# Router logits in four column groups of the tensor engine, and another order of the first loads

## The chip, the cores and the metric

The kernel runs on one core of a Trainium2 chip. The metric is the device time of one execution in microseconds (us), as the median of several runs. The engines are TensorE (PE, matmuls; its weight loads are shown apart as PEld), VectorE (DVE), ScalarE (ACT), GpSimd (POOL) and SyncE (SP), which here only issues DMAs. PE reads SBUF and writes PSUM.

## The reference

One encoder block over a sequence of 1024 tokens with 1024 channels, in fp32:

```python
mod = silu(c) @ w_ada + b_ada                     # 6 parts of 1024
sh1, sc1, g1, sh2, sc2, g2 = split(mod, 6)

h = rmsnorm(x, norm_mix_g) * (1 + sc1) + sh1
u_f, q, k, v = split(h @ w_in)                    # 512 | 512 | 128 | 128 columns
q, k = rmsnorm per head                           # 8 query heads, 2 key/value heads of 64
y_f = fourier_mix(u_f)                            # 2-D DFT, real part, and a linear map per group
y_a = windowed_gqa(q, k, v, rel_bias, sink)       # +-128 tokens, blocks of 128 queries
x = x + g1 * (concat(y_f, y_a) @ w_out)

h2 = rmsnorm(x, norm_ffn_g) * (1 + sc2) + sh2
aff = softmax(h2 @ w_router)                      # 1024 tokens x 16 experts
g, idx = top_k(aff.T, 128)                        # each expert picks its 128 tokens
y_e = (silu(h2[idx] @ w_gate) * (h2[idx] @ w_up)) @ w_down * g
x = x + g2 * scatter_add(y_e)
```

## The kernel before

Tokens lie in 8 tiles of 128. The work has four stages.

1. **First pair of tiles** (`t0` to the first `in_order`). SP loads the identity and small rows, `x` tiles 0 and 1 (512 KB each, `load_x`, L223), the modulation weights of `sh1` and `sc1` and the projection weights `w_in` (`load_w`, L317, 640 KB for each of 8 channel chunks, called w0 to w7 here). The modulation weights come in 8 pieces of 1 MB (`load_mod`, L239, two DMAs of 512 KB each); piece 0 belongs to channel chunk 0, piece 1 to chunk 1, and later pieces come in pairs for two chunks. They are called modulation columns here. `mod_mac` (L127) multiplies such a column with silu(c) in four column groups of PE (32 output partitions each); `mod_sum` copies the result out (ACT, L253) and adds the groups with a matmul against ones (L255); `mod_cols` (DVE, L261 to L263) makes the scale `G1c` and shift `sh1c` of the chunk. `rms` (L193 to L196) squares a tile on ACT, makes the power on POOL, and DVE scales the tile (L355). `pair_chunk` transposes a chunk of both tiles (L271), applies scale and shift (ACT, L278, `hf`) and splits it into a rounded part `hh` and a remainder `hl`; `w_hi` and `w_lo` split the weights in the same way (L397, L321). `terms` (L376) is then the projection, three products for each chunk. The in-order pass at the end of this stage (`in_order(t0, *PINNED)`) holds all five engines to the order in which the program is written, so a statement moved in the source is moved in every engine's queue. The raw tiles of the modulation columns are four buffers, filled again as they are used up.
2. **The other six tiles**, one after the other, with the key and query norms and the rest of the modulation in the background.
3. **Attention, Fourier mixing, output projection, router.** Attention goes through 16 units (tile, key/value head), `front` and `back`; `tick` lets a filler advance in between. The filler is the Fourier part first. After unit 4 (`n == NSW`) the pool `p3` is opened and the filler is `filler2`, which takes the tiles through `oproj` (L81 to L83: three matmuls for each of 8 chunks and two halves). In `oproj(t)`, after the fourth chunk of the first half, `tail(t - 1)` makes the router's logits of the tile before: `x2_flip` transposes its residual (L834) and ACT copies it to `x2T` (L835); eight fp32 matmuls with `x2T` as the stationary operand and `wrG` (router weights times the norm's scale, 16 columns) as the moving one (L850) give 128 tokens x 16 logits in PSUM; DVE applies the token's factor (L852), then softmax into `aff`. For the last tile, `oproj(7)` calls `tail(t, 1)`, where the first four of the eight matmuls (L844) are done ahead. `sorter` sorts the affinities of finished tiles on DVE. Order within this stage is that of the tile framework's planner, which ranks instructions by its own costs; only the lines with `issue_after` are tied. `pt()` gives one of two PSUM buffers that transposes, router and others share.
4. **Experts.** `choose` and `gather` pick tokens for expert 0 (a gap for PE), then 16 experts run on PE with weights split by ACT (L86) and DVE (L87), 1 MB loads for each quarter of a matrix, released by buffers, and in program order on all engines.

An fp32 matmul shows as two records on PE and two weight loads on PEld.

Of the kernel before, what the change touches and what calls it, by code (L numbers as in the profile page):

```python
# [11 lines left out]
F32 = mybir.dt.float32  # L12
# [3 lines left out]
AF = mybir.ActivationFunctionType  # L16
OP = mybir.AluOpType
AX = mybir.AxisListType
# [7 lines left out]
NE = 16  # L26
# [19 lines left out]
def block_kernel(ctx: ExitStack, tc: tile.TileContext, t_in, out):  # L46
    nc = tc.nc
    PE, ACT, DVE, POOL, SP = nc.tensor, nc.scalar, nc.vector, nc.gpsimd, nc.sync

    x = t_in["x"][0]  # L50
# [5 lines left out]
    def pool(name, bufs=1, space=None, **kw):  # L56
        if space is None:
            return tc.tile_pool(name=name, bufs=bufs, reuse_waits="tile", **kw)
        return tc.tile_pool(name=name, bufs=bufs, space=space, **kw)
# [4 lines left out]
    def spacer(p, n):  # L64
        if n:
            p.tile([128, n // 4], F32, name=f"spacer{next(spaced)}", bufs=1)
# [6 lines left out]
    def pt(name="pt"):  # L73
        return ps.tile([128, 512], F32, name=name, tag="pt", bufs=2)
# [14 lines left out]
    def raw(shape):  # L89
        return raw1.tile(shape, F32, name="raw", tag="raw")  # L90


    ident = cst.tile([128, 128], F32, name="ident")
# [47 lines left out]
    def drain(g):  # L141
        for _ in g:
            pass
# [46 lines left out]
    def rms(pool_, src, name, tag, bufs, eng=None):  # L190
        junk = pool_.tile([128, D], BF, name="junk", tag=tag, bufs=bufs)
        ss = pool_.tile([128, 1], F32, name=name + "s", bufs=3)
        ACT.activation(junk, src, AF.Square, accum_out=ss)  # L193
        (eng or DVE).tensor_scalar(ss, ss, 1.0 / D, EPS, op0=OP.mult, op1=OP.add)
        rs = pool_.tile([128, 1], F32, name=name + "r", bufs=3)
        POOL.tensor_tensor(rs, ss, mhalf[:, 0:1], op=OP.pow)  # L196
        return rs
# [7 lines left out]
    p1 = p_a.enter_context(pool("p1"))  # L205
# [10 lines left out]
    xs, xr = {}, {}  # L216

    def stage():
        return p1.tile([128, 1280], F32, name="ws", bufs=2)

    def load_x(t):
        xs[t] = p1.tile([128, D], F32, name="xt", bufs=4)
        SP.dma_start(xs[t], x[t * 128:(t + 1) * 128, :])  # L223
# [9 lines left out]
    def load_mod(h):  # L233
        ks, j, n = halves[h]
        w = len(ks) * 128
        u = raw([128, n, 2, w])
        for i, part in enumerate((1, 0)):
            c0 = part * 1024 + ks[0] * 128
            SP.dma_start(u[:, :, i, :], w_ada_v[:, j:j + n, c0:c0 + w])  # L239
        mods[h] = u.rearrange("p j a c -> p j (a c)")  # L240
# [16 lines left out]
    def mod_cols(*ks):  # L257
        mp = msums.pop(ks)
        n = len(ks)
        c = slice(ks[0], ks[0] + n)  # L260
        DVE.tensor_tensor(G1c[:, c], mp[:, 0:2 * n:2], bscc[:, c], op=OP.add)  # L261
        DVE.tensor_tensor(G1c[:, c], G1c[:, c], ng1c[:, c], op=OP.mult)
        DVE.tensor_tensor(sh1c[:, c], mp[:, 2 * n:4 * n:2], bshc[:, c], op=OP.add)  # L263
# [51 lines left out]
    def load_w(kc):  # L315
        r = u_hi.rearrange("p a b -> p (a b)")[:, :1280] if kc % 3 == 2 else stage()
        SP.dma_start(r, w_in_v[:, kc, :])  # L317
        return r
# [8 lines left out]
    SP.dma_start(rows[0:16], b_ada[:, 0:2048].rearrange("l (j p) -> (l j) p", p=128))  # L327
    SP.dma_start(rows[16:24], t_in["norm_mix_g"].rearrange("l (j p) -> (l j) p", p=128))
    SP.dma_start(rows[24:28], t_in["b_fourier"].rearrange("l (j a) d -> (l j) (a d)", a=2))
    load_x(0)  # L330
    load_x(1)
    load_mod(0)
    load_mod(1)
    wraw = {0: load_w(0)}
    load_mod(2)
    load_mod(3)
    wraw[1] = load_w(1)
    wraw[2] = load_w(2)

    rb = p1.tile([32, 8], F32, name="rb")  # L340
# [2 lines left out]
    pw = p_w.enter_context(pool("pw"))  # L343
    for k in range(8):
        w_h[k], w_l[k] = ((pw if k < 4 else p1).tile([128, 1280], F32R, name=f"w{x}{k}") for x in "hl")
    rs0 = rms(p1, xs[0], "x", tag="hf", bufs=2, eng=POOL)
    rs1 = rms(p1, xs[1], "x", tag="hf", bufs=2, eng=POOL)
    p = pt()
    PE.transpose(p[:, :28], rows[:28], ident[:28, :28])
    DVE.tensor_copy(cols.rearrange("p a b -> p (a b)")[:, :28], p[:, :28])  # L350
    DVE.tensor_scalar(bscc, bscc, 1.0, None, op0=OP.add)
    mod_mac(0)
    mod_sum(0)
    for t, r in enumerate((rs0, rs1)):
        DVE.tensor_scalar(xs[t], xs[t], r, None, op0=OP.mult)  # L355
    mod_cols(0)

    bg, ada, dfts = [], [], []

# [79 lines left out]
    p = terms(pair, 0, hs.pop(0), 0)  # L439
# [64 lines left out]
    for m, (t, kc0) in enumerate(seq):  # L504
# [18 lines left out]
        for a in range(4):  # L523
            project((t,), kc0 + a, hs_, a * 128)
            if m == 0 and a == 1:
                DVE.scalar_tensor_tensor(gg, qg, HD ** -0.5, kg, op0=OP.mult, op1=OP.mult)
                p = pt()
# [309 lines left out]
    def tail(t, b0=0):  # L837
        x2, rs = x2s.pop(t)
        p = None
        for b in range(b0, 2):  # L840
            if b0:
                p = pt()
                for kc in range(4):
                    PE.matmul(p[:, :16], x2Ts[t][:, kc, :], wrG[:, kc, :], start=(kc == 0), stop=False)  # L844
            x2_flip(t, b, x2)
            yield
        x2T = x2Ts.pop(t)
        p = p or pt()
        for kc in range(4 * b0, 8):
            PE.matmul(p[:, :16], x2T[:, kc, :], wrG[:, kc, :], start=(kc == 0), stop=(kc == 7))  # L850
        lg = p3.tile([128, 16], F32, name="lg", bufs=2)
        DVE.scalar_tensor_tensor(lg, p[:, :16], rs, cb, op0=OP.mult, op1=OP.add)  # L852
        mx = p3.tile([128, 1], F32, name="mx", bufs=2)
        DVE.tensor_reduce(mx, lg, axis=AX.X, op=OP.max, negate=True)
        sm = p3.tile([128, 1], F32, name="sm", bufs=2)
        ex = p3.tile([128, 16], F32, name="ex", bufs=2)
        ACT.activation(ex, lg, AF.Exp, bias=mx, accum_out=sm)
        rsm = p3.tile([128, 1], F32, name="rsm", bufs=2)
        DVE.reciprocal(rsm, sm)
        after["aff"] = DVE.tensor_scalar(aff[:, t, :], ex, rsm, None, op0=OP.mult)  # L860
        ready.append(t)
        yield

    def router_prep():
        n2 = p3.tile([64, 128], F32, name="sb_", bufs=1)[:24]
        SP.dma_start(n2[0:8], md[1:2, :].rearrange("l (j p) -> (l j) p", p=128))
        SP.dma_start(n2[8:16], md[2:3, :].rearrange("l (j p) -> (l j) p", p=128))
        SP.dma_start(n2[16:24], t_in["norm_ffn_g"].rearrange("l (j p) -> (l j) p", p=128))
        p = pt()
        PE.transpose(p[:, :24], n2, ident[:24, :24])  # L870
        c2 = p3.tile([128, 24], F32, name="c2")
        DVE.tensor_copy(c2, p[:, :24])
        DVE.scalar_tensor_tensor(c2[:, 8:16], c2[:, 8:16], 1.0, c2[:, 16:24], op0=OP.add, op1=OP.mult)
        p = pt()
        for kc in range(8):
            PE.matmul(p[0:1, :16], c2[:, kc:kc + 1], wr[:, kc, :], start=(kc == 0), stop=(kc == 7))
        row = p3.tile([1, 16], F32, name="row")
        DVE.tensor_copy(row, p[0:1, :16])
        DVE.tensor_tensor(wrG, wr, c2[:, 8:16, None].to_broadcast([128, 8, 16]), op=OP.mult)
        p = pt()  # L880
        PE.matmul(p[:, :16], ones[0:1, :128], row, start=True, stop=True)
        DVE.tensor_copy(cb, p[:, :16])
# [94 lines left out]
    ydone, x2s, x2Ts, xts, ylive = {}, {}, {}, {}, [0]  # L977
    fr, qks, ready, sp = {}, {}, [], [None]
    srt = sorter()
    po, p3 = None, None  # L980
# [18 lines left out]
    for n in range(len(units) + 2):  # L999
        if n == NSW:  # L1000
            for _ in fill[0]:
                for g in lateq:
                    next(g, None)
            for g in lateq:
                drain(g)
            p_f.close()
            p_u.close()
            po = p_c.enter_context(pool("po"))
            p3 = p_c.enter_context(pool("p3", side="right"))
            sp[0] = p3  # L1010
            spacer(p3, 0)
            g1_r, sh2_r, G2_r = (p3.tile([128, D], F32, name=n_) for n_ in ("g1_r", "sh2_r", "G2_r"))
            wr, wrG = (p3.tile([128, 8, NE], F32, name=n_) for n_ in ("wr", "wrG"))
            cb = p3.tile([128, NE], F32, name="cb")
            load_x2(0)
            for i, r in enumerate((g1_r, sh2_r, G2_r)):
                SP.dma_start(r, md[i:i + 1, :].to_broadcast([128, D]))
            wo_h.append(po.tile([128, 2, D], F32R, name="woh3"))
            wo_l.append(po.tile([128, 2, D], F32R, name="wol3"))
            wo_cut()  # L1020
            wo_cut()
            fill = [filler2()]
            SP.dma_start(wr, t_in["w_router"][0].rearrange("(k p) e -> p k e", p=128))
        fg = front(*units[n]) if n < len(units) else iter(())
        bg = back(*units[n - 2]) if n >= 2 else iter(())
        next(fg, None)
        next(bg, None)
        next(fg, None)
        next(bg, None)
        next(bg, None)  # L1030
        drain(fg)
        for g in lateq:
            for _ in range(9):
                next(g, None)
        if n + 1 < len(units):
            qprep(*units[n + 1])
            tick()
        drain(bg)
# [283 lines left out]
    for k0, n in ((0, 2), (2, 2), (4, 4)):  # L1322
        p = pt()
# [119 lines left out]
```

## Time and profile before

| | us |
|---|---|
| median of 3 runs (lowest, highest) | 993.34 (992.99, 994.31) |
| profiled execution, whole | 994.39 |
| its span, first to last instruction | 992.1 |
| PE busy in the span | 938.7 |
| DVE, ACT, POOL busy | 788.6, 626.2, 403.3 |
| mean granted TensorE clock | 0.978 |

In the rows, `L850 PE MATMUL pt<-wrG,x2T 128*128 128x16 f32 x112` reads: line 850, engine PE, output tile `pt` from `wrG` and `x2T`, a 128x128 stationary operand, a 128x16 moving one, 112 records; then busy us and the mean ns of one, then the idle time of the engine just before them and what ended it. In rows by time the first two numbers are the start and the busy time in us, and what stands in brackets is the idle time before the row and what ended it. Rows of stretches give the stretch, its length, the busy us of each engine with the number of instructions, then the granted TensorE clock, the share of the DMA engines and GB/s.

### The profile page before, as it was taken

To read this page: it belongs to the slowest core of one execution; us is meant where nothing else is said; L and a number is where in the kernel's file an instruction comes from. 1 tells how busy PE (TensorE), PEld (TensorE's weight loads), DVE (VectorE), ACT (ScalarE), POOL (GpSimd) and SP (SyncE) were. 2 spreads that over 40 slices of the span, in tenths; PEclk is the share of its full clock that TensorE was granted. 3 is DMA by queue.
4 is the path that set the end of the run, shared out by engine and by line. 5 is a ranking of instruction groups with operands and counts; after the bars stand their busy time and mean duration, and the time that the engine had idled before them with its cause. 6 is when DMAs were issued, how large, how long until landed. Compare 5 with 4: busy or idle time off the path is not lost.

```text
span 992.1 us, 13155 instructions
## 1 busy us (share of the span) xinstructions
PE 938.7 (95%) x4737; PEld 745.1 (75%) x4737; DVE 788.6 (79%) x1237; ACT 626.2 (63%) x831; POOL 403.3 (41%) x239
## 2 busy tenths in 40 slices
PE   4999999979999999599899999999999999999996
PEld 2678776747787777358788888888888888888885
DVE  1336787778767969889879988988998898899894
ACT  2464534666555653137577787787778777777872
POOL 1007465100000000101348769767876976782201
PEclk9999999989999999599899999999999999999998
DMA  9977566362222148799989999999999999999922
GB/s 290 329 259 271 176 213 226 120 190 79 75 75 96 61 145 309 283 405 371 378 307 398 384 385 410 386 386 399 397 389 384 410 385 387 401 395 383 386 84 42
DMA packets 91641, 283.95 MB, mean 286 GB/s; under 512 B 8140, under 2 KB 25728, under 8 KB 91448
## 3 DMA queue, kind: packets, MB, share of 16 engines
q1 hardware_dynamic: 86712, 266.32, 70.6%
q0 software_dynamic: 4864, 16.80, 6.6%
q8 instruction: 37, 0.61, 0.2%
q14 instruction: 28, 0.23, 0.1%
HBM read 263.79 MB, written 21.40 MB: 287 GB/s over the span
## 4 chain that ended last, share of the span: by engine, by line
PE 56%; DMA 1%; DVE 1%; issue 0%; POOLq 0%; ACT 0%; DVEq 0%
PE pa L81 17%; PE pa L83 17%; PE pa L82 17%; PE pt L1290 3%; PE pa L1249 2%; DMA out_dram<-ys,idx 1%; DMA xe<-h2d,idx 0%; DVE wl L87 0%; PE pt L1271 0%; PE pt L1325 0%; POOLq L1439 0%; DVE oneh L1263 0%; DVE ys L1307 0%; PE pa L1135 0%; DVE t1l L87 0%
## 5 line engine op out<-in xcount | busy, mean ns | idle before, releaser
L87 DVE TENSOR_TENSOR wl<-raw,wh 128x2048 fp32r<-128x2048 f32 (+1 forms) x189 | 422.4, 2266 | 55.8 <-ACT wh L86 54.8
L86 ACT ACTIVATE wh<-raw 128x2048 fp32r<-128x2048 f32 (+1 forms) x189 | 355.3, 1896 | 74.9 <-PE pa L82 66.6
L1263 POOL TENSOR_SCALAR oneh<-tri_f,pos 128x128 bf16<-128x128 f32 x96 | 210.5, 2206 | 15.2 <-PE pt L1271 14.7
L81 PE MATMUL pa<-wh,t1h 128*128 128x512 f32 x384 | 151.4, 394 | 0.0
L83 PE MATMUL pa<-wl,t1h 128*128 128x512 f32 x384 | 149.6, 390 | 0.0
L82 PE MATMUL pa<-wh,t1l 128*128 128x512 f32 x384 | 149.5, 389 | 0.0
L81 PE MATMUL pa<-wh,t0h 128*128 128x512 f32 x360 | 143.6, 399 | 0.0
L83 PE MATMUL pa<-wl,t0h 128*128 128x512 f32 x360 | 141.3, 392 | 0.0
L82 PE MATMUL pa<-wh,t0l 128*128 128x512 f32 x360 | 141.2, 392 | 0.0
L803 POOL TENSOR_TENSOR rs<-ss,mhalf 128x1 f32<-128x1 f32 x8 | 4.4, 553 | 214.6 <-DVE ss L801 189.5
L83 PEld LDWEIGHTS pa<-wl,t1h 128*128 128x128 f32 x384 | 72.1, 188 | 15.1
L82 PEld LDWEIGHTS pa<-wh,t1l 128*128 128x128 f32 x384 | 72.2, 188 | 14.3
L81 PEld LDWEIGHTS pa<-wh,t1h 128*128 128x128 f32 x384 | 72.1, 188 | 14.3
L83 PEld LDWEIGHTS pa<-wl,t0h 128*128 128x128 f32 x360 | 68.2, 189 | 14.4
L82 PEld LDWEIGHTS pa<-wh,t0l 128*128 128x128 f32 x360 | 68.3, 190 | 13.8 <-issue 0.2
L81 PEld LDWEIGHTS pa<-wh,t0h 128*128 128x128 f32 x360 | 68.3, 190 | 13.7 <-issue 0.2
L1275 POOL DMA_INDIRECT xe<-h2d,idx x16 | 18.2, 1139 | 141.2 <-DVE gt L1280 133.6
L1305 POOL TENSOR_TENSOR ys<-ys,g_r 128x512 f32<-128x512 f32 x28 | 50.0, 1802 | 46.1 <-ACT ys L1304 46.1
L1308 POOL DMA_INDIRECT out_dram<-ys,idx x15 | 49.3, 3288 | 46.0 <-DVE ys L1307 41.8
L717 ACT ACTIVATE pT<-pt 128x512 f32<-128x512 f32 x44 | 25.9, 596 | 30.9 <-PE pt L715 30.8
L376 PE MATMUL pu<-wh,hh 128*128 128x512 f32 x128 | 42.8, 419 | 2.3 <-ACT hh L86 2.2
L689 DVE CUSTOM_DVE_ANT_0 sb<-lg,bias,sink 128x384 f32<-128x384 f32 (+1 forms) x64 | 35.4, 580 | 12.0 <-PE pt L715 6.5
(322 smaller groups left out, 1637.0 us busy)
## 6 DMA issues: line engine op xcount, KB each, us to landing
raw<-in_w_gate_dram SPq DMA_DIRECT2D x64, 1024.0 KB, 9.2
raw<-in_w_up_dram SPq DMA_DIRECT2D x64, 1024.0 KB, 8.9
raw<-in_w_down_dram SPq DMA_DIRECT2D x63, 1024.0 KB, 9.2
raw<-in_w_ada_dram SPq DMA_DIRECT2D x16, 1024.0 KB, 7.6
raw<-in_w_ada_dram SPq DMA_DIRECT2D x16, 512.0 KB, 8.7
xt<-in_x_dram SPq DMA_DIRECT2D x8, 512.0 KB
raw<-in_w_out_dram SPq DMA_DIRECT2D x4, 1024.0 KB, 4.9
raw<-in_x_dram SPq DMA_DIRECT2D x8, 512.0 KB
```

Source lines behind the costliest of these rows:

```text
L81: PE.matmul(o, lh, rh, start=start, stop=False)
L82: PE.matmul(o, ll, rh, start=False, stop=False)
L83: return PE.matmul(o, lh, rl, start=False, stop=stop)
L86: ACT.activation(hi, src, AF.Copy)
L87: return (eng or DVE).tensor_tensor(lo, src, hi.bitcast(F32), op=OP.subtract)
L376: PE.matmul(acc[:, :c1 - c0], lhs, r[kc][:, c0:c1], start=first, stop=(kc == 7 and r is w_l), skip_group_check=c0 == 1024)
L689: DVE.tensor_tensor_reduce(sb[:, :wid], lg[:, :wid], bias[:, kv * 4 + i, j0:j0 + wid], 1.0, sk[:, i:i + 1], op0=OP.add, op1=OP.max, accum_ ...
L717: ACT.activation(pT, pp, AF.Copy)
L1263: (POOL if t < shared else DVE).tensor_scalar(oneh[:, t, :], slots, pos[:, t, e:e + 1], None, op0=OP.is_equal)
L1290: PE.transpose(p[:, k * 128:k * 128 + 128], src[:, (4 * b + k) * 128:(4 * b + k + 1) * 128], ident)
L1305: POOL.tensor_tensor(ys[:, cs_], ys[:, cs_], g2_r[:, cs_], op=OP.mult)
L1308: POOL.indirect_dma_start(out=out2, out_offset=bass.IndirectOffsetOnAxis(ap=idx[:, :1], axis=0), in_=ys, in_offset=None, compute_op=OP.add)
```

## The change

Two edits. In the router, all tiles but the last take another form: `wrG` is widened to 32 columns (the upper 16 zero) and becomes the stationary operand; `x2T` is the moving one with 128 columns; chunk `kc` goes to column group `kc % 4` (32 PSUM partitions each), so each group adds up two chunks. ACT copies the 128x128 result to `gsum`, and one more matmul with `gsum` as stationary operand and `gsel` (four 16-column identities, one below the other 32 rows apart) adds the groups and turns the result back into tokens x experts. `gsel` is made once, from the identity.

In the first stage, modulation column 0 is loaded ahead of the x tiles, w0 and w1 move ahead of modulation columns 1 and 2, and the squares and scalings of the two x tiles are written behind `mod_mac(0)` and `mod_sum(0)`, with `mod_cols(0)` between the two tiles.

```diff
     SP.dma_start(rows[24:28], t_in["b_fourier"]...)
+    load_mod(0)
     load_x(0)
     load_x(1)
-    load_mod(0)
+    wraw = {0: load_w(0)}
     load_mod(1)
-    wraw = {0: load_w(0)}
+    wraw[1] = load_w(1)
     load_mod(2)
     load_mod(3)
-    wraw[1] = load_w(1)
     wraw[2] = load_w(2)
...
-    rs0 = rms(p1, xs[0], "x", tag="hf", bufs=2, eng=POOL)
-    rs1 = rms(p1, xs[1], "x", tag="hf", bufs=2, eng=POOL)
...
     mod_mac(0)
     mod_sum(0)
-    for t, r in enumerate((rs0, rs1)):
+    for t in range(2):
+        r = rms(p1, xs[t], "x", tag="hf", bufs=2, eng=POOL)
         DVE.tensor_scalar(xs[t], xs[t], r, None, op0=OP.mult)
-    mod_cols(0)
+        if t == 0:
+            mod_cols(0)
...
         x2T = x2Ts.pop(t)
-        p = p or pt()
-        for kc in range(4 * b0, 8):
-            PE.matmul(p[:, :16], x2T[:, kc, :], wrG[:, kc, :], start=(kc == 0), stop=(kc == 7))
+        if b0:
+            for kc in range(4, 8):
+                PE.matmul(p[:, :16], x2T[:, kc, :], wrG[:, kc, :16], start=False, stop=(kc == 7))
+        else:
+            p = pt()
+            for kc in range(8):
+                g = 32 * (kc % 4)
+                PE.matmul(p[g:g + 32, :128], wrG[:, kc, :], x2T[:, kc, :], start=(kc < 4), stop=(kc >= 4))
+            gs_ = p3.tile([128, 128], F32, name="gsum", bufs=1)
+            ACT.activation(gs_, p[:, :128], AF.Copy)
+            p = pt()
+            PE.matmul(p[:, :16], gs_, gsel[:, :16], start=True, stop=True)
...
-        DVE.tensor_tensor(wrG, wr, c2[:, 8:16, None].to_broadcast([128, 8, 16]), op=OP.mult)
+        DVE.tensor_tensor(wrG[:, :, :NE], wr, c2[:, 8:16, None].to_broadcast([128, 8, 16]), op=OP.mult)
...
-            wr, wrG = (p3.tile([128, 8, NE], F32, name=n_) for n_ in ("wr", "wrG"))
+            wr = p3.tile([128, 8, NE], F32, name="wr")
+            wrG = p3.tile([128, 8, 32], F32, name="wrG")
+            gsel = p3.tile([128, 32], F32, name="gsel")
+            POOL.memset(wrG, 0.0)
+            DVE.tensor_reduce(gsel, ident.rearrange("p (g e) -> p e g", g=4), axis=AX.X, op=OP.add)
```

More of the change, by code (lines that the diff above doesn't have):

```diff
@@ L843, in tail @@
                 for kc in range(4):
-                    PE.matmul(p[:, :16], x2Ts[t][:, kc, :], wrG[:, kc, :], start=(kc == 0), stop=False)
+                    PE.matmul(p[:, :16], x2Ts[t][:, kc, :], wrG[:, kc, :16], start=(kc == 0), stop=False)
             x2_flip(t, b, x2)
```

## The prediction

> **What bounds the kernel now.** I read the page first (busy shares, slices, the chain that ended last), then busy time by stretches, then the groups and the order of time at the two places that the diff touches.
>
> ```profile
> span 992.1 us, 13155 instructions
> ...
> PE 938.7 (95%) x4737; PEld 745.1 (75%) x4737; DVE 788.6 (79%) x1237; ACT 626.2 (63%) x831; POOL 403.3 (41%) x239
> ...
> PE   4999999979999999599899999999999999999996
> ...
> PE 56%; DMA 1%; DVE 1%; issue 0%; POOLq 0%; ACT 0%; DVEq 0%
> ```
>
> TensorE (PE) is busy 95% of the span; its low slices are the start (first digit), the place where attention opens its second stage, and the routing before the experts (the lone 5). The stretches say it sharper:
>
> ```profile
> core 0: us, PE busy (x) PEld busy (x) DVE busy (x) ACT busy (x) POOL busy (x), PEclk, DMA share, GB/s
> 210.00:220.00 10.00, 8.36 (x32) 5.60 (x32) 7.01 (x23) 4.60 (x14) 0.00 (x0) 0.66 0.81 255
> 215.00:390.00 175.00, 174.09 (x1022) 135.06 (x1022) 133.86 (x461) 95.63 (x266) 4.47 (x9) 0.99 0.30 110
> 480.00:490.00 10.00, 6.43 (x40) 5.31 (x39) 10.00 (x15) 6.44 (x5) 0.00 (x0) 0.93 1.02 382
> 600.00:700.00 100.00, 100.00 (x483) 82.80 (x482) 89.39 (x63) 77.78 (x57) 75.13 (x35) 1.00 1.03 392
> ```
>
> From 215 to 390 us, where all seven changed router passes lie, PE is busy 174.09 of 175 us: PE time saved there is time saved. The experts behind are PE's too (100 of 100 us); one stretch, 480 to 490, is VectorE's (DVE 10.00). Both hang on when the experts begin, so a shift ahead of them should arrive at the end: the weight loads are released by buffers, which move with PE.
>
> **The router, before.** One tile's pass is 8 fp32 matmuls, two records each, with a 128x128 weight load for 16 columns:
>
> ```profile
> L850 PE MATMUL pt<-wrG,x2T 128*128 128x16 f32 x112 | 14.0, 261 | 0.2
> L850 PEld LDWEIGHTS pt<-wrG,x2T 128*128 128x128 f32 x112 | 13.6, 191 | 1.9 <-ACT x2T L835 1.0 <-issue 0.4
> L835 ACT ACTIVATE x2T<-pt 128x512 f32<-128x512 f32 x15 | 8.8, 595 | 5.1 <-PE pt L834 5.1
> ...
> 252.33 1.85 PE L850 MATMUL pt<-wrG,x2T 128*128 128x16 f32 x16
> 254.04 0.48 PE L83 MATMUL pj<-wol,yah 128*128 128x512 f32 x1
> ...
> 270.80 1.96 PE L850 MATMUL pt<-wrG,x2T 128*128 128x16 f32 x16
> 272.61 0.48 PE L82 MATMUL pj<-woh,yal 128*128 128x512 f32 x1
> ```
>
> 112 records are seven tiles of 16. A pass holds PE until the next matmul starts: 1.71 us (252.33 to 254.04) and 1.81 (270.80 to 272.61); I take 1.74. That is 0.11 a record, what a weight load costs, not what 16 columns cost.
>
> **The router, after.** The router weights become the stationary operand (32 columns, four groups side by side), the tokens stream (128 columns), ACT copies the four partial sums out, and one more matmul adds them. The trace has the same form elsewhere:
>
> ```profile
> 419.95 17.17 PE pa L1249 x40
> 439.89 0.87 PE pt L1290 x8
> ...
> 39.06 0.28 PE L376 MATMUL pv<-wh,hl 128*128 128x256 f32 x1
> 39.27 1.92 PE L127 MATMUL px<-raw,c_act 128*32 128x512 f32 x16
> ...
> 259.90 0.40 PE L83 MATMUL pj<-wol,yh 128*128 128x512 f32 x1
> 260.22 1.51 PE L728 MATMUL yp<-pT,vf 128*64 128x256 f32 x12
> 261.67 0.50 PE L81 MATMUL pj<-woh,yah 128*128 128x512 f32 x1
> ...
> L388 ACT ACTIVATE vf<-pv 128x128 f32<-128x128 f32 x5 | 1.4, 284 | 0.0
> ```
>
> - Groups: a 512-column fp32 record takes 17.17/40 = 0.429 us alone, so 16 of them 6.9; in four groups (L127) they took 1.92, that is four deep, 4 x 0.429 = 1.72, and 0.2 over. The groups do run side by side. A 128-column record takes 0.87/8 = 0.109, so the new pass is 4 x 0.109 = 0.43.
> - Going in and out: the two-group matmuls at 260.22 begin 0.32 after a matmul that else takes 0.23, and hold 1.45 (to 261.67) for six deep of half a 512 record, 1.29: 0.09 + 0.16 = 0.25.
> - Adding matmul: two records at 0.11 = 0.23, no cheaper, since it loads 128x128 weights (L850's own price).
> - The new wait: PE needs ACT's copy (0.28, the 128x128 copy of L388) in front of the adding matmul. What is queued behind it is the output projection and the attention matmuls of that tile; the logits (DVE) wait for it. Existing waits of this kind: L850's weight loads stood 1.9 us over seven passes, 1.0 of it for ACT's x2T; the order is the planner's, which fits other matmuls between. I put 0.2 a tile. Bounds: 0, and 0.7 (0.17, which is what a busy row of PE runs beyond the next start, and 0.28 copy and a third of a 0.6 us ACT piece, nothing between).
> - Sum: 0.43 + 0.25 + 0.23 + 0.2 = 1.11 for 1.74, 0.63 saved, times seven 4.4 us. Ends: no stall and 0.17 for the mode, 0.91 x 7 = 6.4; stall of 0.7, 0.13 x 7 = 0.9.
> - The skill has a rule that speaks against it: the Trainium skill, TensorEngine Tiling (Array Packing), Tiling Modes, says that changing the tiling mode drains TensorE. The 0.25 above agrees that a change costs; were it a drain of 0.17 at each side, the sum would be 3.7 instead of 4.4.
> - Beside other work: ACT gets 7 x 0.28 = 2.0 us, with 95.6 of 175 busy. DVE's and POOL's one-off pieces (the 128x128 reduction to `gsel`, the memset of `wrG`, the strided write of `wrG`) fall in the gap where attention's second stage opens; DVE is 7.01 of 10 there (210 to 220), and I cost them nothing; uncovered, up to 0.5 us. Each pass takes one more of the two shared PSUM buffers `pt`, for about as long as it held the one before: nothing, or some of the 0.7. The last tile keeps its form, so the chain into the routing is unchanged.
>
> **The first loads.** In order of time:
>
> ```profile
> xt<-in_x_dram SPq DMA_DIRECT2D x6, 512.0 KB
> raw<-in_w_ada_dram SPq DMA_DIRECT2D x16, 512.0 KB, 8.7
> ws<-in_w_in_dram SPq DMA_DIRECT2D x6, 640.0 KB, 6.6
> ...
> 2.80 0.83 SPq L223 DMA_DIRECT2D xt<-in_x_dram  x2
> 7.91 1.06 ACT L193 ACTIVATE junk<-xt 128x1024 bf16<-128x1024 f32 x1 [0.17 <-DMA xt<-in_x_dram]
> 12.57 1.93 PE L127 MATMUL px<-raw,c_act 128*32 128x256 f32 x16 [8.25 <-DMA raw<-in_w_ada_dram]
> 16.69 1.94 PE L127 MATMUL px<-raw,c_act 128*32 128x256 f32 x16
> 17.75 1.27 ACT L397 ACTIVATE wh<-ws 128x1280 fp32r<-128x1280 f32 x1 [2.81 <-DMA ws<-in_w_in_dram]
> 19.51 0.42 ACT L86 ACTIVATE hh<-hf 128x256 fp32r<-128x256 f32 x1
> 19.98 0.79 PE L376 MATMUL pu<-wh,hh 128*128 128x512 f32 x1 [1.35 <-ACT hh L86]
> 26.31 1.92 PE L127 MATMUL px<-raw,c_act 128*32 128x512 f32 x16
> ...
> 10.00:20.00 10.00, 5.41 (x39) 2.54 (x39) 1.19 (x5) 2.60 (x5) 0.15 (x1) 1.00 1.11 332
> 31.20:34.60 3.40, 3.40 (x11) 2.71 (x11) 0.68 (x4) 0.02 (x1) 0.00 (x0) 0.51 1.09 348
> ...
> 43.52 1.28 ACT L397 ACTIVATE wh<-ws 128x1280 fp32r<-128x1280 f32 x1 [1.66 <-DMA ws<-in_w_in_dram]
> 45.49 0.42 ACT L86 ACTIVATE hh<-hf 128x256 fp32r<-128x256 f32 x1
> 47.24 0.62 PE L376 MATMUL pu<-wh,hh 128*128 128x512 f32 x2
> ```
>
> The DMA engines are full (share 1.11 in 10 to 20 us) and SP issues ahead of them, so what counts is how many bytes stand ahead. Modulation column 0 (two DMAs of 512 KB) loses the two x tiles, 1 MB, ahead of it. A column behind them took 4.7 us (7.91 to 12.57); issued at 2.8 in their place, with a µs or two until the first bytes flow, it should land near 9. The x tiles slip behind it, to about 10 and 11.5; the squares, powers and scalings, now in order behind the column on ACT, DVE and POOL, are done near 16, the first `hh` near 17.5. But column 1, whose matmuls stand ahead of the first product on PE, now comes after w0: the bytes up to it are just those that before ended with w0, which landed at 17.75. So its matmuls move from 16.69 to 17.75, end at 19.7, and the first product starts there, not at 19.98: 0.3 gained, of the 3 that the earlier column promises. From 17.75 on PE has no gap, where before it had 1.35 us (the row at 19.98), and its slow start (0.79 for a 512-column record that takes 0.40 at 259.90) may end sooner: by up to 2.2 us (17.75 against 19.98), half of which is gained, 1.1; I take 0.5. The cap: w4 stands behind the same bytes in both orders, lands at 43.5, and leads to `hh` at 45.91, needed at 47.24: PE can't run ahead by more than 1.3. **Sum 0.8**, ends +1.3 and -1.7: a gap in other places can cost a second stretch at half clock like 31.2 to 34.6 (clock 0.51), half of 3.4. Columns 2 and 3 go behind w1, 640 KB or some 2 us; PE took them at 26.31 without waiting for a DMA, and I cost that at nothing; if they had only just landed, up to 1 us, within the ends. The Trainium skill, TensorE: Matmul & The Clock Gate, part 1, has such windows of 3.4 us running freely; the 3.40 us row agrees. By that rule the half-speed start ends at a window's edge, so the 0.5 would be 0 or 1.7, which keeps within the ends.
>
> **Sum.** 4.4 + 0.8 = 5.2 us off the profiled execution: it took 994.39 us (span 992.1 and 2.3 around it), so 989.2. The runs' median, 993.34, stands 1.05 below that execution; against it, 988.1.
>
> **Rivals.**
> - The adding matmul stalls PE for good (the other side): ACT works first in, first out, and a 0.6 us piece with its 0.2 read stands ahead of each copy: 0.17 + 0.8 + 0.28 = 1.25 a tile, nothing between. Then 0.91 + 1.25 = 2.16 for 1.74, 2.9 lost in seven, less the 0.8: 995.4. It loses from a stall of 0.83 on. For it: a chain PE, ACT, PE in each tile. Against it: the same chain through x2T cost PE under 0.3 a pass.
> - The saving is eaten: stalls near 0.7, so 0.9, and the start gives nothing because column 1 is late: 992.4, no change that can be told.
> - More than that: no stall and the start at its cap, 6.4 + 1.3 = 7.7: 985.6. For it: PE's queue always has other matmuls in this stage. Against it: nothing in the trace enters and leaves the groups for free.
>
> **How the numbers follow.** Forecast 0.55 (its own range 985.9 to 991.3), more 0.15, eaten 0.18, stall 0.12. The likeliest gives 988.1. The measurement tells about 0.2% (2 us) from no change, so faster 0.70, same 0.18, slower 0.12. The range takes in the best end and the eaten case with the planner's reordering of the attention stage around it: 984.8 to 994.0.
>
> **What would show it.** Right: eight column-group matmuls of about 0.6 us, a 0.28 us copy, two records behind it, PE still at 174 of 175 in a stage some 4 us shorter; the first product at 19.7 with column 1's matmuls waiting for their DMA near 17.75; the experts with PE at 100 of 100 as before. Wrong: PE idle for ACT ahead of the adding matmul; a first product past 20; or the stage shorter and the gap ahead of the experts longer.

## The result and the profile after

The changed kernel takes 985.86 us as the median of 6 runs (985.47 to 986.48); the kernel before, on the same chip, 994.34 (6 runs, 992.99 to 994.83). The ratio is 0.9918, 95% interval [0.9905, 0.9931]: 8.5 us less, where 5.2 were forecast. The profiled executions are 994.39 us before and 986.08 after. A second comparison on another chip gave 984.89 against 993.90, ratio 0.9916 [0.9902, 0.9929].

The page of the changed kernel; its first lines, and TensorE's in the 40 slices:

```profile
span 984.3 us, 13194 instructions
...
PE 934.3 (95%) x4751; PEld 737.0 (75%) x4751; DVE 788.5 (80%) x1238; ACT 628.5 (64%) x838; POOL 403.9 (41%) x240
...
PE   4999999989999998799899999999999999999996
```

PE has 4.4 us less busy time, but the span is 7.8 us shorter, so some 3 us of idle time on PE went too. That alone says that the forecast, which counted mainly work, left something out.

Busy time by stretches of the changed kernel (same columns as before the change: PE, PEld, DVE, ACT, POOL, granted TensorE clock, DMA share, GB/s):

```profile
205.00:215.00 10.00, 8.30 (x30) 5.66 (x29) 7.90 (x27) 6.75 (x22) 0.00 (x0) 0.72 0.72 227
210.00:385.00 175.00, 174.06 (x1063) 130.58 (x1062) 141.65 (x491) 104.37 (x288) 4.52 (x9) 0.99 0.35 123
600.00:700.00 100.00, 100.00 (x487) 82.86 (x486) 89.71 (x65) 78.37 (x59) 75.14 (x35) 1.00 1.03 392
```

The same first stretch in the kernel before:

```profile
205.00:215.00 10.00, 6.47 (x30) 4.12 (x27) 8.79 (x29) 7.69 (x25) 0.00 (x0) 0.85 0.72 217
```

PE is still full through the router passes (174.06 of 175) and through the experts (100 of 100), as forecast. Not forecast is the first row: where attention's second stage opens, PE is busy 8.30 of 10 us and was 6.47. The busy time alone doesn't say that more was done there: both rows have 30 matmul records, and the granted clock is 0.72 in the one and 0.85 in the other, so some of these records only took longer. The waits, shown below, tell more.

**The router.** The groups of the changed kernel (busy us, mean ns of one; then the idle time before them) in the stretch with the seven passes:

```profile
L856 PE MATMUL pt<-x2T,wrG 128*32 128x128 f32 x112 | 5.7, 282 | 0.0
L860 PE MATMUL pt<-gsel,gsum 128*128 128x16 f32 x14 | 2.1, 225 | 0.0
L860 PEld LDWEIGHTS pt<-gsel,gsum 128*128 128x128 f32 x14 | 2.1, 188 | 1.2 <-ACT gsum L858 1.2
L858 ACT ACTIVATE gsum<-pt 128x128 f32<-128x128 f32 x7 | 1.9, 278 | 5.9 <-PE pt L856 5.9
```

The 112 records fell from 14.0 to 5.7 us of PE time. The adding matmul (L860) has no idle time on PE before it: the weight loads waited 1.2 us over seven passes for ACT's copy, beside other matmuls. One pass in order of time shows what covers the copy:

```profile
249.92 0.34 PE L687 MATMUL lg<-klo,qk 128*128 128x384 f32 x1
250.19 0.64 PE L856 MATMUL pt<-x2T,wrG 128*32 128x128 f32 x16
250.76 0.51 PE L83 MATMUL pj<-wol,yah 128*128 128x512 f32 x1
250.90 0.28 ACT L858 ACTIVATE gsum<-pt 128x128 f32<-128x128 f32 x1 [0.66 <-PE pt L856]
251.10 0.33 PE L686 MATMUL lg<-khi,qk 128*128 128x384 f32 x1
251.28 0.35 PE L860 MATMUL pt<-gsel,gsum 128*128 128x16 f32 x2
251.47 0.42 PE L687 MATMUL lg<-klo,qk 128*128 128x384 f32 x1
```

The planner put a projection matmul (L83) and an attention matmul (L686) between the groups and the adding matmul. The copy ends at 251.18; PE gets to L860 at 251.28. The groups hold PE for 0.57 us (250.19 to 250.76) and begin 0.27 after the attention matmul ahead of them. In the kernel before, the same pass, which began at 252.33, stood behind the same attention matmul, 0.17 after its start:

```profile
252.16 0.34 PE L687 MATMUL lg<-klo,qk 128*128 128x384 f32 x1
```

**The start.** The changed kernel's first stage in order of time, PE with ACT's first `hh` and a later split of projection weights:

```profile
8.92 1.94 PE L127 MATMUL px<-raw,c_act 128*32 128x256 f32 x16 [4.54 <-DMA raw<-in_w_ada_dram]
...
16.76 0.42 ACT L86 ACTIVATE hh<-hf 128x256 fp32r<-128x256 f32 x1
17.55 1.93 PE L127 MATMUL px<-raw,c_act 128*32 128x256 f32 x16 [1.49 <-DMA raw<-in_w_ada_dram]
19.41 1.22 PE L376 MATMUL pu<-wh,hh 128*128 128x512 f32 x2
...
42.52 1.28 ACT L397 ACTIVATE wh<-ws 128x1280 fp32r<-128x1280 f32 x1 [1.57 <-DMA ws<-in_w_in_dram]
```

Column 0 comes at 8.92 (forecast: near 9), column 1's matmuls wait for their DMA to 17.55 (17.75), and the first product starts at 19.41 (19.7). `hh` is there at 17.18, 2.2 us before it is used: column 1 is what holds the first product, as forecast. The later weights came a microsecond earlier in this execution (42.52, before 43.52), so the cap that was set on the start at 1.3 us rested on a landing that itself moved.

**The opening of attention's second stage.** VectorE and TensorE of the kernel before, then of the changed kernel, in order of time:

```profile
210.90 1.23 DVE L87 TENSOR_TENSOR wol<-raw,woh 128x1024 fp32r<-128x1024 f32 x1
212.57 0.69 DVE L87 TENSOR_TENSOR yl<-yt,yh 128x512 fp32r<-128x512 f32 x1
213.32 0.80 PE L82 MATMUL pj<-woh,yl 128*128 128x512 f32 x1 [1.55 <-DVE yl L87]
```

```profile
211.15 0.38 DVE L1027 TENSOR_REDUCE gsel<-ident 128x32 f32<-128x128 f32 x1
211.44 0.68 DVE L87 TENSOR_TENSOR yl<-yt,yh 128x512 fp32r<-128x512 f32 x1
...
212.40 0.63 PE L82 MATMUL pj<-woh,yl 128*128 128x512 f32 x1
212.76 1.22 DVE L87 TENSOR_TENSOR wol<-raw,woh 128x1024 fp32r<-128x1024 f32 x1
```

Here is the part that the forecast missed. With the reduction to `gsel` and the memset of `wrG` added at this place, the planner ordered two VectorE instructions the other way round: `yl` (the remainder of the first tile's Fourier half, which the output projection needs at once) now comes ahead of a split of `w_out`, for which PE shows no wait in the changed kernel. PE's wait of 1.55 us for `yl` is gone. The order of PE's own matmuls from 214 us on is another too; the experiments come back to that.

How long each part took, from starts of instructions in one profiled execution of each kernel. Second column: the first matmul `yp<-pT` of attention to the 33rd, which spans the opening of the second stage. Third: from there to the logits of the seventh router pass. Fourth: on to the gather for expert 0. Fifth: from there to the end of the last matmul.

| us | first product | opening | seven passes | to the gather | experts |
|---|---|---|---|---|---|
| before | 19.98 | 31.93 | 148.91 | 23.29 | 574.74 |
| changed | 19.41 | 30.72 | 143.29 | 23.42 | 574.33 |
| changed, second profile | 19.81 | 30.72 | 143.33 | 23.33 | 574.50 |

The gain was made at the opening (1.2) and in the seven passes (5.6), with 1.0 us ahead of both (the first `yp` is at 204.58 and 203.59); the last two columns hardly move. Each row is one execution, and the opening holds 6.8 us at half clock in all three (the last section has what that does).

### The profile page after: what moved, and what is told of

It is laid out like the page before. It is cut to its first block, busy times and chain, and to the rows that moved or that the text cites. A ratio compares the mean times of both kernels' runs of the same rounds, so it can differ in the third digit from the quotient of the medians.

```text
span 984.3 us, 13194 instructions
## 1 busy us (share of the span) xinstructions
PE 934.3 (95%) x4751; PEld 737.0 (75%) x4751; DVE 788.5 (80%) x1238; ACT 628.5 (64%) x838; POOL 403.9 (41%) x240
## 4 chain that ended last, share of the span: by engine, by line
PE 56%; DMA 1%; DVE 1%; issue 0%; POOLq 0%; ACT 0%; DVEq 0%
PE pa L81 17%; PE pa L83 17%; PE pa L82 17%; PE pt L1304 3%; PE pa L1263 2%; DMA out_dram<-ys,idx 1%; DVE wl L87 0%; DMA xe<-h2d,idx 0%; PE pt L1285 0%; PE pt L1339 0%; POOLq L1453 0%; DVE oneh L1277 0%; DVE ys L1321 0%; PE pa L1149 0%; DVE t1l L87 0%
## 5 line engine op out<-in xcount | busy, mean ns | idle before, releaser
L83 PE MATMUL pa<-wl,t1h 128*128 128x512 f32 x384 | 149.6, 390 | 0.0
L83 PE MATMUL pa<-wl,t0h 128*128 128x512 f32 x360 | 141.2, 392 | 0.0
L83 PEld LDWEIGHTS pa<-wl,t1h 128*128 128x128 f32 x384 | 72.1, 188 | 15.2
L83 PEld LDWEIGHTS pa<-wl,t0h 128*128 128x128 f32 x360 | 68.1, 189 | 14.5
L278 ACT ACTIVATE hf<-pt,sh1c,G1c 128x128 f32<-128x128 f32 (+1 forms) x56 | 22.6, 482 | 34.9 <-PE pt L271 34.9
```

What stands on the lines that cost most here:

```text
L83: return PE.matmul(o, lh, rl, start=False, stop=stop)
L278: ACT.activation(hf[:, a * w:a * w + w], tp[:, a * w:a * w + w], AF.Identity, scale=G1c[:, kc:kc + 1], bias=sh1c[:, kc:kc + 1])
```

## The experiments

Three causes were to be told apart: the new form of the router's matmuls, the start, and the order that the planner made at the opening. Each ratio below is to the kernel before on the same chip, with its 95% interval.

### The router's edit alone

The first stage is put back to the kernel before:

```diff
-    load_mod(0)
     load_x(0)
     load_x(1)
+    load_mod(0)
...
+    rs0 = rms(p1, xs[0], ...)
+    rs1 = rms(p1, xs[1], ...)
```

> The router edit alone, with the first loads as before. The order of instructions on TensorE is that of the changed kernel, but for the first stage. Theory A (the parts add up; start 1.0 us, the rest 7): 7.2 to 7.6 us under before. Theory B (the start is worth more than the 1.0 us by which the traces differ at 200 us, since it shifts the work against the clock's windows of 3.4 us where the third stage opens): 5 to 6 us under before.

986.75 us (5 runs, 985.42 to 988.60) against 994.15; 0.9928 [0.9915, 0.9941], 7.4 us less. The router's edit brings nearly all of it, and more than the 4.4 forecast for it.

### The start alone

The router, with `wrG` of 16 columns and no `gsel`, is that of the kernel before:

```diff
-            for kc in range(8):
-                g = 32 * (kc % 4)
-                PE.matmul(p[g:g + 32, :128], wrG[:, kc, :], x2T[:, kc, :], ...)
...
+        for kc in range(4 * b0, 8):
+            PE.matmul(p[:, :16], x2T[:, kc, :], wrG[:, kc, :], ...)
```

> The new first loads alone, with the router as before. Theory A: 0.8 to 1.2 us under before, all of it there at 62 us and none added later. Theory B: more than 2 us under before, gained where the third stage opens.

993.33 us (11 runs, 991.43 to 994.10); 0.9989 [0.9980, 0.9998], 0.8 us less by the medians (1.1 by the ratio, 0.2 to 2.0 by its interval), what the forecast had for the start. With the 7.4 that makes 8.2 of the 8.5: the two edits add up. The profiled execution, at 991.43 the quickest of the eleven, runs PE's instructions in the order of the kernel before and is ahead of its profile by 2.2 us at 62 us and by 2.9 at the end; as one execution it decides nothing.

### Layout, memset and `gsel`, with the old matmuls and the old loads

```diff
-                PE.matmul(p[g:g + 32, :128], wrG[:, kc, :], x2T[:, kc, :], ...)
-            ACT.activation(gs_, p[:, :128], AF.Copy)
-            PE.matmul(p[:, :16], gs_, gsel[:, :16], ...)
+        for kc in range(4 * b0, 8):
+            PE.matmul(p[:, :16], x2T[:, kc, :], wrG[:, kc, :16], start=(kc == 0), stop=(kc == 7))
```

`wrG` keeps its 32 columns and `gsel` is made but not used.

> Old loads and the old router matmuls, but with the 32-column wrG, its memset and the gsel reduction (unused). Up to the first router pass TensorE's order is that of the changed kernel. Theory A (part of the gain is not the router's form but another order of the planner where the third stage opens, in which VectorE makes yl ahead of a weight split and TensorE no longer waits 1.5 us for it): 1 to 2.5 us under before. Theory B (the gain is the router's form alone): within 0.5 us of before.

991.09 us (11 runs, 989.50 to 994.53); 0.9980 [0.9971, 0.9990]: 2.0 us less by the ratio, 3.1 by the medians, for a kernel that only does a little more than before. VectorE at the opening:

```profile
210.26 0.39 DVE L1017 TENSOR_REDUCE gsel<-ident 128x32 f32<-128x128 f32 x1
210.57 0.68 DVE L87 TENSOR_TENSOR yl<-yt,yh 128x512 fp32r<-128x512 f32 x1
211.71 1.22 DVE L87 TENSOR_TENSOR wol<-raw,woh 128x1024 fp32r<-128x1024 f32 x1
```

It has the changed kernel's order, and a gain with it, within Theory A's 1 to 2.5 by the ratio and above it by the medians. The seven passes took 148.33 us here (before 148.91), so the new matmuls themselves are worth 148.33 - 143.29 = 5.0 us. The stretch of the changed kernel has two more projection matmuls of 0.23 us in it, so for the same work it is nearer 5.5. The runs of this kernel and of the router alone, 991.09 - 986.75, say 4.3.

### All eight chunks in one column group

```diff
-                g = 32 * (kc % 4)
+                g = 0
...
-            ACT.activation(gs_, p[:, :128], AF.Copy)
-            PE.matmul(p[:, :16], gs_, gsel[:, :16], ...)
+            ACT.activation(gs_[:32], p[:32, :128], AF.Copy)
+            PE.matmul(p[:, :16], gs_[:32], gsel[:32, :16], ...)
```

> The changed kernel with all eight router matmuls of a tile in one column group (32 PSUM partitions), the copy and the adding matmul over these 32 partitions alone. Theory A (the groups run side by side and that is where the router's gain is): a pass goes from 0.8 to 16 x 0.109 = 1.74 us, 7 x 1.0 = 6 to 8 us slower than the changed kernel. Theory B (the gain is from loading 32 instead of 128 columns of weights, the groups matter little): within 2 us of the changed kernel.

995.79 us (12 runs, 991.90 to 996.81); 1.0010 [1.0000, 1.0020]: 10.1 us above the changed kernel by the medians' distances to before, 9.1 by the ratios, more than the 6 to 8 of Theory A. Its router matmuls and its adding matmul:

```profile
L856 PE MATMUL pt<-x2T,wrG 128*32 128x128 f32 x112 | 13.9, 274 | 0.2
L860 PE MATMUL pt<-gsel,gsum 32*128 32x16 f32 x14 | 2.7, 268 | 0.0
```

13.9 us for the 112 records, as much as the old form's 14.0: a whole pass holds PE for 1.86 us, where four groups hold it for 0.57. Swapping the operands alone gains nothing; that four groups run side by side is the whole gain (13.9 to 5.7). The adding matmul over 32 partitions isn't cheaper but dearer here: it holds PE for 0.32 us, in the changed kernel for 0.14 to 0.20, which is some 1.2 us in seven passes and much of what lies above Theory A's range.

### The kernel before, with `yl` ahead of the second split

```diff
+    with tc.issue_after(ylo[0].ins):     # ylo[0]: the instruction that makes yl of tile 0
         wo_cut()
```

> The kernel before, with one tie of order added: VectorE makes yl of tile 0 ahead of the second split of the last output weights. Nothing else is changed. Theory A (what the unused layout of e3 gained is this order: TensorE's 1.5 us wait for yl goes): 1 to 2.5 us under before. Theory B (the gain of e3 came from elsewhere in the planner's order): within 0.7 us of before.

991.32 us (5 runs, 989.99 to 993.15) against 994.61; 0.9965 [0.9951, 0.9979], 3.3 us less, above the 1 to 2.5 of Theory A. VectorE at the opening:

```profile
211.47 0.69 DVE L87 TENSOR_TENSOR yl<-yt,yh 128x512 fp32r<-128x512 f32 x1
212.07 1.22 DVE L87 TENSOR_TENSOR wol<-raw,woh 128x1024 fp32r<-128x1024 f32 x1
```

Nothing of the change is in this kernel but the order that follows from the one tie. With it the planner gave PE the very order of the third experiment, tile for tile in all 4737 matmul records. So that order is the cause of what the third experiment gained, not the layout or the memset. It is more than two instructions, though: against the kernel before, PE's records are in another order at 23 places between 214 and 274 us. PE's wait for `yl` (1.5 us before, none here) is the part that can be seen. How much of the 3.3 us is that wait, and how much the other order of PE's matmuls, no run tells apart.

### The changed kernel, with `yl` put back behind the split

```diff
-            wo_cut()
+            wlast = wo_cut()
+            tc.add_manual_dep(ylo[0].ins, wlast.ins.name, NOSYNC, reason="order")
```

> The changed kernel, with yl of tile 0 tied behind that weight split, which is the order of before there. Theory A: the wait of about 1.5 us for yl is back, 1 to 2.5 us slower than the changed kernel, that is 6 to 7.5 us under before. Theory B: as the changed kernel, 8 us under before.

987.17 us, but spread from 984.25 to 989.79 (5 runs); 0.9934 [0.9921, 0.9948]. Too wide to set against the changed kernel's 0.9918, so it was run again beside it.

> The changed kernel once more, as the base of the two beside it. Every theory: 985.9 us, 8.5 less than the kernel before (8.0 to 9.0).

984.89 us (5 runs, 984.55 to 986.97) against 993.90, as told above.

> Changed kernel with the order at the third stage's opening put back by hand (yl behind the last split). Theory A (the order is worth 1 to 3 us of the 8.5): 1.0 to 3.0 us above the changed kernel beside it. Rival (the order's gain in the other runs came from something else that the reduction of gsel moved): within 0.5 us of it.

987.42 us (5 runs, 987.13 to 988.99); 0.9940 [0.9926, 0.9953]. On the same chip that is 2.5 us above the changed kernel, with no run of the one inside the range of the other. What PE waited for from 200 to 222 us (total, times, longest; the longest three), in this kernel and then in the changed kernel beside it:

```profile
PE pt L715 <- DVE sb L704: 2.0, 2, 1.8
PE pj L82 <- DVE yl L87: 1.8, 1, 1.8
PE pt L715 <- ACT u_hi L637: 1.4, 1, 1.4
```

```profile
PE pt L715 <- DVE sb L704: 1.7, 2, 1.5
PE pt L715 <- ACT u_hi L637: 1.4, 1, 1.4
PE pt L715 <- ACT pT L717: 0.8, 1, 0.8
```

The wait for `yl` is back, 1.8 us, and the opening takes 32.18 us instead of 30.72. Here too PE's matmuls from 214 us on are in another order along with `yl`. So the order is worth 2.5 us by these runs (1.5 at the opening by the trace), 2.0 to 3.5 in the kernel before by the ratios of the two experiments above. The 3.1 and 3.3 by the medians lie within that.

### The copy twice

```diff
-            ACT.activation(gs_, p[:, :128], AF.Copy)
+            for _ in range(2):
+                ACT.activation(gs_, p[:, :128], AF.Copy)
```

> The changed kernel with ScalarE's copy of the four partial sums done twice in a row in each of the seven passes, so that the adding matmul is released 0.28 us later. Theory A (other matmuls lie between, the wait costs TensorE nothing): within 1 us of the changed kernel. Theory B (TensorE stands behind the copy): 7 x 0.28 = 2 us slower than it, or more.

986.59 us (5 runs, 985.49 to 987.11); 0.9915 [0.9901, 0.9928], the changed kernel's own ratio. Its groups:

```profile
L859 ACT ACTIVATE gsum<-pt 128x128 f32<-128x128 f32 x14 | 3.9, 278 | 6.2 <-PE pt L856 5.9
L861 PE MATMUL pt<-gsel,gsum 128*128 128x16 f32 x14 | 2.5, 254 | 0.0
L861 PEld LDWEIGHTS pt<-gsel,gsum 128*128 128x128 f32 x14 | 2.1, 188 | 1.5 <-ACT gsum L859 1.5
```

Twice the copies (14, 3.9 us on ACT), and PE's idle time before the adding matmul is still 0.0. That doesn't show room of 0.28 us in the changed kernel's own order (there the copy ended 0.10 ahead of L860): the planner ordered PE's matmuls otherwise and put one or two more of them ahead of the adding matmul; in the pass at 250 us these are an attention and a projection matmul that had followed it. The seven passes took 144.01 us, 0.7 more than in the changed kernel, and none of it is PE waiting for ACT: the adding matmul holds PE for 0.21 to 0.22 us in six of the seven passes, where it was 0.14. So the longer chain brings no stall; the order made around it can still cost a little, less than these runs resolve.

### Column 1's matmuls behind the first product

```diff
-    column(1)
     p = terms(pair, 0, ...)
+    next(p)
+    column(1)
```

> The changed kernel with the matmuls of modulation column 1 written behind the first group of products, which need only column 0 and w0. Theory A (column 1 is what the first product waits for, and w4 then caps the lead at about 1 us more): the first product near 17.3 us instead of 19.4, 0.3 to 1 us under the changed kernel at the end. Theory B (the first products were held by the split of x or w0, not by column 1): the first product stays at 19 or later, no gain.

985.64 us (4 runs, 983.69 to 987.47); 0.9902 [0.9887, 0.9917]. In its profiled execution the first product was at 18.74, not much earlier than the changed kernel's, since column 0's matmuls themselves had started 1.5 us later (10.44); it came right behind `hh`, which was done at 18.69. Run again beside the changed kernel:

> Changed kernel with column 1's sixteen matmuls behind the first product's group. Theory A (the 2.2 us that the first product gains behind column 0's landing reaches the end): 1.0 to 2.2 us below the changed kernel beside it. Rival (the first stage ends by its loads of weights, so the gain is given back): within 0.5 us of it.

984.13 us (4 runs, 982.63 to 984.65); 0.9902 [0.9887, 0.9917]. PE in order of time:

```profile
8.88 1.94 PE L127 MATMUL px<-raw,c_act 128*32 128x256 f32 x16 [4.69 <-DMA raw<-in_w_ada_dram]
...
17.20 1.22 PE L376 MATMUL pu<-wh,hh 128*128 128x512 f32 x2 [1.16 <-ACT hh L86]
...
19.63 1.60 PE L127 MATMUL px<-raw,c_act 128*32 128x256 f32 x16
```

With column 0 where the changed kernel has it (8.88), the first product starts at 17.20 instead of 19.41, right behind `hh`. So column 1 was the holder. What reaches the end is 0.8 us by the medians beside the changed kernel, below the 1.0 to 2.2 and above the 0.5 that were expected, and the intervals overlap: not settled.

### Router passes in one piece

In the changed kernel five of the seven passes go through PE in two pieces, since the first four chunks need only the first half of `x2T`. This version, on top of the one before, takes the second half's chunks first:

```diff
-            for kc in range(8):
+            for kc in (4, 5, 6, 7, 0, 1, 2, 3):
...
-                PE.matmul(p[g:g + 32, :128], ..., start=(kc < 4), stop=(kc >= 4))
+                PE.matmul(p[g:g + 32, :128], ..., start=(kc >= 4), stop=(kc < 4))
```

> Changed kernel with column 1's matmuls behind the first product's group and, in the seven router passes, the chunks of the second half first (4 to 7, then 0 to 3), so that a pass waits for both halves of x2T and goes through PE in one piece instead of in two (in the changed kernel five of seven passes go in two). Theory A (each piece pays its own way into and out of the column groups, some 0.25 us): the stretch of the seven passes, 143.3 us in the changed kernel, shrinks by 0.9 to 1.4 us, and the kernel runs 9.5 to 11.5 us below the kernel before. Rival (the first piece filled a time in which PE would wait for the second half of x2T, or the copy and the adding matmul lose their cover): the stretch within 0.4 us of 143.3 or longer, the kernel 8.0 to 9.5 us below the kernel before.

986.48 us (5 runs, 983.79 to 987.72) against 993.82; 0.9923 [0.9910, 0.9937], 7.3 us less, under even the rival's 8.0 to 9.5. Its group, and PE's waits from 215 to 385 us:

```profile
L857 PE MATMUL pt<-x2T,wrG 128*32 128x128 f32 x112 | 4.9, 279 | 0.0
```

```profile
PE pt L835 <- issue: 0.6, 1, 0.6
```

Six of seven passes are whole now and the records hold PE for 4.9 us instead of 5.7, but the stretch of the seven passes is 143.16 us, only 0.1 to 0.2 shorter (0.4 for the same work, as it has one projection matmul of 0.23 us more in it), and the kernel is not faster. Within the stretch PE shows no wait. The new wait of 0.6 us before a transpose of the residual comes at 381.0, behind the end of the stretch at 377.7, and takes back about what was saved; what makes it stays open. The expected gain of 0.9 to 1.4 did not come. Of all versions the one with the products first has the lowest ratio, twice 0.9902, but not clearly below the changed kernel's.

## Why the prediction was right, and where not

- **Direction and range: right.** 985.86 lies in 984.8 to 994.0, at the edge of the likeliest case's own range (985.9 to 991.3). It is close to the time of the rival "more than that" (985.6), but not by that rival's mechanism: that had all 7.7 us from the router and the start. With the old order put back the changed kernel took 987.42, 6.0 (ratio) to 6.5 us (medians) under the kernel before. That is what the router and the start bring, against the 5.2 forecast; the rest of the 8.5 is an order that no term of the sum had, and that it was a gain and not a loss was luck.
- **PE's time is the kernel's time there: right.** PE is full in the stretch before and after, and the experts kept their 574 us, so what was saved ahead of them arrived.
- **The groups: right in size.** 0.43 for the columns and 0.25 for going in and out made 0.68. A whole pass measures 0.57 of holding PE plus 0.10 ahead (0.27 less 0.17, from the rows above): 0.67. Five passes go in two pieces, mostly of 0.36 each, and pay the way in twice; worked out from the starts of all seven, with 0.10 ahead of each piece as an estimate, the mean is 0.85. The prediction showed only whole passes; in the kernel before four of the seven already went in two pieces. The Trainium skill, TensorEngine Tiling (Array Packing), Tiling Modes, says that a change of mode drains TensorE; the 0.24 beyond the 0.43 agrees with a cost of that kind, and two drains of 0.17 would have been 0.34.
- **The stall: mis-sized.** "I put 0.2 a tile" for ACT's copy; it measures 0.0, and 0.0 with twice the copies. Both times the planner filled the time with matmuls of the same stage. With that the stalled rival and the eaten one fall: both needed PE with nothing to do behind the groups.
- **The adding matmul: a little mis-sized.** 0.23 forecast, 0.14 to 0.20 by the next matmul's start.
- **Together** a pass costs 0.85 + 0.15 = 1.00 instead of 1.11, so 1.76 - 1.00 = 0.76 is saved instead of 0.63, 5.3 in seven (1.76 is the mean of the seven passes before); by the lengths of the stretch it is 5.0 to 5.5.
- **The last tile: right.** The way from the seventh pass to the gather took 23.29 and 23.42 us.
- **The start: right in sum, not shown in its parts.** 0.8 forecast, 0.8 by the runs of that edit alone; its 0.3 for the first product measured 0.57 in these executions. The other 0.5, from an earlier end of the slow clock, isn't shown: the slow clock ended at 24.3 us before and at 26.4 and 23.6 in the two profiles of the changed kernel. See the last section.
- **The one-off pieces at the opening, "I cost them nothing": the step that failed.** PE shows no wait for the reduction to `gsel`, 0.38 us of VectorE. But the planner's order is part of the program, and with these pieces in it VectorE's and PE's orders at the opening came out otherwise: 2.0 to 3.5 us, the largest part of the miss. The prediction named a reordering only as a reason for a wider range, and shows nothing of what PE waited for at that place, where the wait for `yl` was to be seen.
- **Sum:** 5.0 to 5.5 (router) + 0.8 (start) + 2.0 to 3.5 (order) = 7.8 to 9.8, measured 8.5.

## What to carry to other kernels

Where a matmul has few columns and its time is that of its weight loads, make the small operand the stationary one and spread the contraction over column groups; without the groups the swap gave nothing. A chain over another engine made PE wait for nothing here, since the planner had independent matmuls to put into it, so look for those before you price a stall. Where a planner orders the instructions, compare the order of every engine around the place where an instruction is added, and read the waits of the bounding engine there first: here a tie of one line in the kernel before brought 3.3 us. And such a tie can turn round far more than the two instructions that it names.

## What the runs showed of the hardware

The granted clock falls to half in stretches that are multiples of 3.4 us (3.4, 6.8, 20.5 and 23.9 in these profiles), and where they lie differs between kernels and executions. In the changed kernel's stretches around the opening:

```profile
203.80:207.20 3.40, 3.40 (x13) 1.58 (x10) 1.45 (x4) 3.33 (x13) 0.00 (x0) 0.51 0.54 146
207.20:210.70 3.50, 1.80 (x11) 1.23 (x10) 3.04 (x15) 0.99 (x4) 0.00 (x0) 0.99 0.53 169
210.70:214.10 3.40, 3.40 (x10) 2.59 (x10) 3.24 (x8) 3.35 (x11) 0.00 (x0) 0.50 1.03 346
```

By its length, a stretch of 3.4 us at half clock costs up to 1.7 us of PE work; that is an estimate. The kernel with the layout alone had none at the opening, which fits its shortest opening (29.07 us; with the same order of PE's records but 6.8 us at half clock, the kernel before with the tie took 30.76):

```profile
205.00:210.00 5.00, 3.04 (x18) 1.96 (x17) 4.36 (x18) 3.69 (x15) 0.00 (x0) 1.00 0.46 131
210.00:215.00 5.00, 4.80 (x23) 3.69 (x22) 4.87 (x13) 3.40 (x11) 0.00 (x0) 1.00 1.00 283
```

The end of the slow start lay anywhere from 19.8 to 26.4 us in the profiled executions. That is in line with the Trainium skill, TensorE: Matmul & The Clock Gate, part 1, by which the windows run freely of the program.

How much this moves a single execution, the kernel with `yl` behind the split shows, which was profiled twice with every engine's instructions in the same order (spans 982.4 and 986.9). In the second profile column 1's matmuls waited for their load to 18.09 us instead of 16.77, and the slow start ended at 24.4 us instead of 19.8; at 62 us it was 2.6 behind. Between 207 and 216 us, where both had 6.8 us at half clock but at other instructions, it lost 0.9 more, and around 390, where it had 23.9 us at half clock instead of 20.5, another 1.0; from there to the end next to nothing. The runs agree: in the kernel with the layout alone the six with a mean granted clock of 0.982 or 0.983 took 989.50 to 991.17 us, the five with 0.977 to 0.980 took 991.02 to 994.53. So an edit worth 1 us needs many runs; one execution's first product or first stage can't show it.

The order at the opening and the clock also go together. None of the 56 runs of the kernel before beside the experiments had a clock above 0.980, and 9 of the 16 runs of the layout kernel and of the kernel before with the tie, which have the new order with the old router matmuls, did. So part of the order's 2.0 to 3.5 us comes with a higher clock; how much isn't shown.
